# A two-layer hybrid decoder trunk: the low half of every weight tile is formed on GpSimd instead of VectorE

## The chip, the cores and the metric

The kernel runs as one program on one core of a Trainium2 chip. The metric is the device time of one execution in microseconds (us), the median of three runs. Five engines work beside each other, each with its own queue of instructions that it takes strictly in order: TensorE (PE in the profile, with its weight loads as PEld), VectorE (DVE), ScalarE (ACT), GpSimd (POOL) and SyncE (SP), which here only issues DMAs. They wait for each other by semaphores.

## The reference, cut to what matters

Each of the two layers normalises its input, multiplies it by one wide input projection, runs four token mixers on slices of the result (retention, a gated linear recurrence, a diagonal state space with a scan, and a Mamba-2 style recurrence), gates and concatenates the four outputs, and multiplies them by an output projection that is added to the residual. The prompt has 2048 tokens of width 1024; beside it go 8 single tokens with states of their own.

```python
hn = rms_norm(x, norm_w)
proj = (hn @ w_in).astype(f32)            # 1024 x 3332
...                                       # four mixers, 256 columns each
mixed = jnp.concatenate([o_ret, o_hgrn, o_s5, o_m2], axis=-1).astype(x.dtype)
x_out = x + mixed @ w_out                 # 1024 x 1024
```

All of it is float32. The kernel keeps that precision in the two large products by splitting each operand into a high part, rounded to the matmul's reduced float32 type (fp32r), and a low part, the rest: `hi*hi + lo*hi + hi*lo`, three matmuls in place of one.

## The kernel before, in words

The prompt is worked through in blocks of 512 tokens, four to a layer, eight in all. For a block the program runs the input projection in four pieces (`gemm_A`, `gemm_H`, `gemm_M`, `gemm_S`), the mixers (`mix_A`, `mix_H`, `mix_M`, `mix_S`) and the output projection (`out_proj`). The mixers are generators. After each weight tile of a projection the program hands out a few of their steps, so that TensorE's order, which is written out by hand, alternates between a dozen projection matmuls and a mixer's small ones.

The order on the other engines is not written by hand. A scheduler places their instructions by priority and by its own idea of when each is ready; weight tiles have the priority offset `WPRI`, evacuations of finished banks `EPRI`. What a queue holds is fixed when the program is built.

A weight tile comes through a small pipeline, in `gemm` (narrow, lines 606 to 618) and in `gemm_wide` (lines 683 to 691). A DMA fetches 256 KB into a `wr` tile, of which there are 6; ScalarE writes the high half, rounded, into a `wh` tile, of which there are 5; VectorE subtracts the two and writes the low half:

```python
S.copy(hl[:, 0, 0:512], raw[:, 0:512])                        # L688: high half, ScalarE
V.tensor_tensor(hl[:, 1, 0:512], raw[:, 0:512],
                hl[:, 0, 0:512].bitcast(F32), ALU.subtract)   # L689: low half, VectorE
```

There are 296 tiles from `gemm_wide` (L688 and L689) and 248 from `gemm` (L615 and L616), 544 in all. TensorE uses a tile in 12 or 24 matmuls on lines 695, 633 and 628. Both inputs of the subtraction lie in SBUF, as does its output.

GpSimd has little to do before the change. The letters in `GS = 'rpdmwf'` choose what it does: the sums of the rotary embedding in `gemm_A` (L1133 and L1134, four pairs to a block), a product and the diagonals at the start of `mix_H` (L1270, L1281), two products in `mix_S` (L1452 and L1455), the decay masks of `mix_M` (L1585, eight to a block), and parts of the set-up of a layer (L299, L303). Everything else elementwise is VectorE's: it reads the finished banks (tiles `gb` and `mb` in PSUM), and runs the chains of the mixers, the inverse square roots (L227 to L233) among them. The buffers named `half` and `big` are shared by all mixers.

Of the kernel before, what the change touches and what calls it, by code (L numbers as in the profile page):

```python
# [11 lines left out]
F32 = mybir.dt.float32  # L12
# [4 lines left out]
ALU = mybir.AluOpType  # L17
# [96 lines left out]
def trunk_kernel(ctx: ExitStack, tc: tile.TileContext, A: dict):  # L114
    nc = tc.nc
    V, G, S, T = nc.vector, nc.gpsimd, nc.scalar, nc.tensor
# [29 lines left out]
    def nm(s):  # L146
        uid[0] += 1
        return f"{s}_{uid[0]}"
# [32 lines left out]
    def mbank():  # L181
        return mps.tile([P, 512], F32, name=nm("mb"), tag="mb")
# [415 lines left out]
    def gemm(lhs, w, c0, mode, evac, dec=None, tail=None, ks=(0, 1, 2, 3), late=False):  # L598
        n = 256 + (4 if tail is not None else 0)
        per = 2 if (mode == "T" and tail is None) else 1  # L600
        nb = 4 if tail is not None else 2
        banks = [gps.tile([P, 512], F32, name=nm("gb"), tag="gb") for _ in range(nb)]
        dbank = mbank() if dec is not None else None
        raws, hls = [], []

        def load(ki):
            k2 = ks[ki]
            with tc.high_priority(offset=WPRI):
                hl = whp.tile([P, 2, 2, 260], F32R, name=nm("wh"), tag="wh")
                raw = wrp.tile([P, 2, 260], F32, name=nm("wr"), tag="wr")  # L610
                rows = w[2 * k2 * P : 2 * (k2 + 1) * P].rearrange("(k p) c -> p k c", p=P)
                nc.sync.dma_start(raw[:, :, 0:256], rows[:, :, c0 : c0 + 256])
                if tail is not None:
                    nc.sync.dma_start(raw[:, :, 256:260], rows[:, :, tail : tail + 4])
                S.copy(hl[:, 0, :, :n], raw[:, :, :n])  # L615
                V.tensor_tensor(hl[:, 1, :, :n], raw[:, :, :n], hl[:, 0, :, :n].bitcast(F32), ALU.subtract)  # L616
            hls.append(hl)
            raws.append(raw)

        def out(i):  # L620
            with tc.high_priority(offset=EPRI):
                evac(i, banks[i][:, 0 : per * 256].rearrange("p (t c) -> p t c", t=2) if per == 2 else banks[i])

        def t_pass(ki, tt):
            for k in range(2):
                o = banks[tt // per][:, (tt % per) * 256 : (tt % per) * 256 + n]
                for pi, (a, c) in enumerate(((1, 0), (0, 1), (0, 0))):
                    T.matmul(o, lhs[2 * ks[ki] + k][:, a, tt * P : (tt + 1) * P], hls[ki][:, c, k, :n],  # L628
                             start=(ki == 0 and k == 0 and pi == 0 and tt % per == 0), stop=(ki == 3 and k == 1 and pi == 2 and tt % per == per - 1))

        def f_pass(ki, k, i):
            for pi, (a, c) in enumerate(((1, 0), (0, 1), (0, 0))):
                T.matmul(banks[i], hls[ki][:, a, k, i * P : (i + 1) * P], lhs[2 * ks[ki] + k][:, c, :],  # L633
                         start=(ki == 0 and k == 0 and pi == 0), stop=(ki == 3 and k == 1 and pi == 2))

        def dec_pass(ki):
            for j in range(4 if dec is not None else 0):
                T.matmul(dbank[32 * j : 32 * j + 8, :n], dec[0]()[:, 2 * ks[ki - 1 + j // 2] + j % 2, :], raws[ki - 1 + j // 2][:, j % 2, :n],
                         start=(ki == 1), stop=(ki == 3))

        if late:
            for ki in range(4):
                load(ki)
            for tt in range(4):
                for ki in range(4):
                    t_pass(ki, tt)
                if tt % per == per - 1:
                    out(tt // per)
                if tt == 3:
                    for ki in (1, 3):  # L650
                        dec_pass(ki)
                    if dec is not None:
                        dec[1](n, dbank)
                yield
            return
        for ki in range(4):
            load(ki)
            if mode == "T":
                for tt in range(4):
                    t_pass(ki, tt)  # L660
                    if ki == 3 and tt % per == per - 1:
                        out(tt // per)
            elif ki < 3:
                for k in range(2):
                    for i in range(2):
                        f_pass(ki, k, i)
            else:
                for i in range(2):
                    for k in range(2):
                        f_pass(ki, k, i)  # L670
                    out(i)
            if ki % 2 == 1:
                dec_pass(ki)
            if ki == 3 and dec is not None:
                dec[1](n, dbank)
            yield

    def gemm_wide(lhs, w, c0, evac, dec=None, ks=tuple(range(KT)), pre=None, lead=2):
        banks = [gps.tile([P, 512], F32, name=nm("gb"), tag="gb") for _ in range(4)]
        dbank = mbank() if dec is not None else None  # L680
        raws, hls = [], []

        def load(kt):
            with tc.high_priority(offset=WPRI):
                hl = whp.tile([P, 2, 520], F32R, name=nm("wh"), tag="wh")
                raw = wrp.tile([P, 520], F32, name=nm("wr"), tag="wr")
                nc.sync.dma_start(raw[:, 0:512], w[ks[kt] * P : (ks[kt] + 1) * P, c0 : c0 + 512])
                S.copy(hl[:, 0, 0:512], raw[:, 0:512])  # L688
                V.tensor_tensor(hl[:, 1, 0:512], raw[:, 0:512], hl[:, 0, 0:512].bitcast(F32), ALU.subtract)  # L689
            raws.append(raw)  # L690
            hls.append(hl)

        def t_pass(kt, tt):
            for pi, (a, c) in enumerate(((1, 0), (0, 1), (0, 0))):
                T.matmul(banks[tt], lhs[ks[kt]][:, a, tt * P : (tt + 1) * P], hls[kt][:, c, 0:512],  # L695
                         start=(kt == 0 and pi == 0), stop=(kt == KT - 1 and pi == 2))

        def dec_pass(kt):
            if dec is not None and kt % DW == DW - 1:
                for k in range(kt - DW + 1, kt + 1):  # L700
                    j = k % 4
                    T.matmul(dbank[32 * j : 32 * j + 8, :], dec[0]()[:, ks[k], :], raws[k][:, 0:512], start=(k < 4), stop=(k >= 4))

        for kt in range(KT - 2):
            load(kt)
            for tt in range(4):
                t_pass(kt, tt)
            dec_pass(kt)
            if pre is not None and lead and kt >= KT - 2 - lead:
                pre(kt - KT + 2 + lead)  # L710
            yield
        load(KT - 2)
        load(KT - 1)
        for tt in range(4):
            t_pass(KT - 2, tt)
            t_pass(KT - 1, tt)
            with tc.high_priority(offset=EPRI):
                evac(tt, banks[tt])
            if pre is not None and lead and tt + lead < 4:
                pre(tt + lead)  # L720
            if tt == 1:
                yield
        dec_pass(KT - 2)
        dec_pass(KT - 1)
        if dec is not None:
            dec[1](512, dbank)
        yield
# [394 lines left out]
    def gemm_A(L, B):  # L1122
# [27 lines left out]
        def ev2(tt, ps):  # L1150
            S.copy(B.rv[:, tt, :], ps[:, 0:256])
            S.activation(B.rg[:, tt, :], ps[:, 256:512], AF.Silu)

        yield from gemm_wide(B.hn, w, C_RV, ev2, dec=B.dec and B.dec.chunk("rv"))
        yield from gemm_wide(B.hn, w, C_RQ, ev1, dec=dec, pre=pre1)

    def mix_A(L, B):
# [895 lines left out]
```

## Time and profile before

| | |
|---|---|
| time, median of 3 runs | 2244.28 us (2241.43 to 2245.09) |
| the profiled execution | 2245.02 us, its span 2243.2 us |
| TensorE busy | 2118.9 us, 94% |
| VectorE busy | 1669.3 us, 74% |
| ScalarE busy | 1034.2 us, 46% |
| GpSimd busy | 239.5 us, 11% |
| mean granted TensorE clock | 0.98 |

The span runs from the first to the last instruction of the profile; 1.8 us of the execution lie outside it. A share of busy time says how much of the span an engine was executing; the time in which its queue stood still because the instruction at its head was waiting does not count as busy, and the view of waits shows it instead.

### The profile page before, as it was taken

How to read it: one execution, taken by the hardware profiler on the slowest of the kernel's cores; microseconds unless marked ns; L12 is line 12 of the kernel's file. 1: busy time of each engine (PE TensorE's matmuls, PEld its weight loads, DVE VectorE, ACT ScalarE, POOL GpSimd, SP SyncE). 2: the span in 40 equal slices, each digit the busy share in tenths (PEclk: the TensorE clock that was granted, in tenths of full speed). 3: DMA queues.
4: the chain of work that ended last, by engine and by line, in shares of the span. 5: the costliest groups of instructions: out<-in, count | busy, mean ns of one | idle time of the engine just before them, and what ended most of it. 6: DMA issues, size and time to landing. Idle time of an engine off the chain costs nothing. (4 is left out here: it accounts for less than half of the span.)

```text
span 2243.2 us, 41062 instructions
## 1 busy us (share of the span) xinstructions
PE 2118.9 (94%) x15031; PEld 1712.8 (76%) x15031; DVE 1669.3 (74%) x4614; ACT 1034.2 (46%) x1889; POOL 239.5 (11%) x212
## 2 busy tenths in 40 slices
PE   7999989999999999999999998999899899999996
PEld 7778767776777877788877876777677678878786
DVE  6888666898749977787747867489985687748774
ACT  7434433456333564346453453444634245454343
POOL 0112011000210002201100011000120001100100
PEclk9999999999999999999999999999999999999999
DMA  6324633236524364374533335334652253431272
GB/s 213 104 66 120 182 104 118 90 108 203 143 67 143 94 196 121 115 167 126 179 97 112 95 113 165 99 109 119 202 154 78 86 163 101 156 92 50 68 260 94
DMA packets 263354, 284.41 MB, mean 127 GB/s; under 512 B 88752, under 2 KB 183616, under 8 KB 263152
## 3 DMA queue, kind: packets, MB, share of 16 engines
q1 hardware_dynamic: 263152, 281.79, 42.4%
q8 instruction: 118, 1.93, 0.4%
q14 instruction: 84, 0.69, 0.1%
HBM read 245.52 MB, written 31.99 MB: 124 GB/s over the span
## 5 line engine op out<-in xcount | busy, mean ns | idle before, releaser
L695 PE MATMUL gb<-wh,hn 128*128 128x512 f32 x2208 | 542.1, 400 | 3.4 <-DVE half L1650 2.3
L633 PE MATMUL gb<-hn,wh 128*128 128x512 f32 x1920 | 485.9, 406 | 10.3 <-DVE wh L616 6.9
L695 PEld LDWEIGHTS gb<-wh,hn 128*128 128x128 f32 x2208 | 409.9, 188 | 109.1 <-issue 11.6
L633 PEld LDWEIGHTS gb<-hn,wh 128*128 128x128 f32 x1920 | 359.9, 192 | 99.2 <-DVE wh L616 8.1
L689 DVE TENSOR_TENSOR wh<-wr,wh 128x512 fp32r<-128x512 f32 x296 | 215.3, 732 | 242.6 <-ACT wh L688 239.2
L688 ACT CAST wh<-wr 128x512 fp32r<-128x512 f32 x296 | 183.2, 620 | 373.5 <-PE gb L695 193.6
L695 PE MATMUL gb<-wh,mx 128*128 128x512 f32 x1344 | 341.5, 407 | 7.9 <-DVE half L1733 5.8
L695 PEld LDWEIGHTS gb<-wh,mx 128*128 128x128 f32 x1344 | 251.3, 192 | 77.8 <-DVE half L1733 10.1
L615 ACT CAST wh<-wr 128x512 fp32r<-128x512 f32 (+1 forms) x248 | 152.3, 619 | 308.4 <-PE gb L633 83.5
L616 DVE TENSOR_TENSOR wh<-wr,wh 128x512 fp32r<-128x512 f32 (+1 forms) x248 | 183.3, 745 | 77.6 <-ACT wh L615 74.2
L628 PE MATMUL gb<-wh,hn 128*128 128x256 f32 (+1 forms) x1728 | 220.2, 286 | 11.1 <-DVE convc L1524 4.7
L628 PEld LDWEIGHTS gb<-wh,hn 128*128 128x128 f32 x1728 | 211.6, 191 | 15.8 <-issue 9.2
L1585 POOL TENSOR_TENSOR half<-mats,m_lal 128x512 fp32r<-128x512 f32 x64 | 75.5, 1198 | 829.1 <-DVE m_lal L1579 278.8
L1330 DVE COPY_PREDICATED big<-lvl,mb 64x256 f32<-64x256 int32 x192 | 95.3, 537 | 2.5
L1297 ACT COPY zbH<-big 64x512 f32<-64x512 f32 x112 | 70.8, 632 | 48.5 <-PE mb L1306 35.9
L1523 DVE SCALAR_TENSOR_TENSOR big<-gb,vt,big 128x511 f32<-128x511 f32 (+2 forms) x96 | 71.1, 743 | 3.9 <-ACT big L1521 3.5
L1306 PE MATMUL mb<-zbH,big 128*64 128x64 f32 x1536 | 56.9, 229 | 11.0 <-DVE half L1177 5.3
L1306 PEld LDWEIGHTS mb<-zbH,big 128*64 128x64 f32 x1536 | 50.8, 142 | 20.5 <-issue 15.4
L1281 POOL TENSOR_TENSOR big<-mats,h_dg 128x1024 f32<-128x1024 f32 x16 | 30.7, 1942 | 241.8 <-DVE h_dg L1278 197.6
L1482 PE MATMUL mb<-big,big 128*64 128x128 f32 x512 | 40.6, 307 | 15.1 <-DMA big<-s5c 14.7
L628 PE MATMUL gb<-wh,mx 128*128 128x256 f32 x384 | 47.3, 282 | 4.7 <-DVE mx L1505 2.8
L1482 PEld LDWEIGHTS mb<-big,big 128*64 128x64 f32 x512 | 33.6, 155 | 23.7 <-issue 17.0
(497 smaller groups left out, 3091.2 us busy)
## 6 DMA issues: line engine op xcount, KB each, us to landing
wr<-in_w_in SPq DMA_DIRECT2D x416, 256.0 KB
wr<-in_w_out SPq DMA_DIRECT2D x128, 256.0 KB
big<-s5c SPq DMA_DIRECT2D x64, 256.0 KB
xn<-xmid SPq DMA_DIRECT2D x32, 512.0 KB
xn<-in_x_prompt SPq DMA_DIRECT2D x24, 512.0 KB
big<-s5c SPq DMA_DIRECT2D x24, 512.0 KB
xmid<-half SPq DMA_DIRECT2D x44, 256.0 KB
half<-xmid SPq DMA_DIRECT2D x44, 256.0 KB
```

Of the source, the lines that this page charges most:

```text
L615: S.copy(hl[:, 0, :, :n], raw[:, :, :n])
L616: V.tensor_tensor(hl[:, 1, :, :n], raw[:, :, :n], hl[:, 0, :, :n].bitcast(F32), ALU.subtract)
L628: T.matmul(o, lhs[2 * ks[ki] + k][:, a, tt * P : (tt + 1) * P], hls[ki][:, c, k, :n], start=(ki == 0 and k == 0 and pi == 0 and tt % per = ...
L633: T.matmul(banks[i], hls[ki][:, a, k, i * P : (i + 1) * P], lhs[2 * ks[ki] + k][:, c, :], start=(ki == 0 and k == 0 and pi == 0), stop=(ki ...
L688: S.copy(hl[:, 0, 0:512], raw[:, 0:512])
L689: V.tensor_tensor(hl[:, 1, 0:512], raw[:, 0:512], hl[:, 0, 0:512].bitcast(F32), ALU.subtract)
L695: T.matmul(banks[tt], lhs[ks[kt]][:, a, tt * P : (tt + 1) * P], hls[kt][:, c, 0:512], start=(kt == 0 and pi == 0), stop=(kt == KT - 1 and ...
L1306: T.matmul(ps[su, j * 64 : (j + 1) * 64], k[:, j // 4, (j % 4) * P + 64 * u : (j % 4) * P + 64 * u + 64], qz[:, :, j * 64 + 32 * u : j * 6 ...
L1330: V.copy_predicated(stv[p][su, :, nu * u : nu * u + nu, :], mv, ps[su, p * 256 : p * 256 + 256].rearrange("p (c b h) -> p c b h", c=8, h=h))
L1482: T.matmul(ps[64 * hb : 64 * hb + 64, g4 * P : (g4 + 1) * P], lhs, (tq if i else cq)[:, hb, g4], start=(i == 0), stop=(i == 1))
L1523: V.scalar_tensor_tensor(acc[:, 3 - i :], ps[:, : TB - 3 + i], w(i), acc[:, 3 - i :], ALU.mult, ALU.add)
L1585: E('m').tensor_tensor(mms[tt][i].rearrange("p (h t) -> p h t", h=4), tri[:, None, :].to_broadcast([P, 4, P]), lal[:, i, tt, :][:, :, None ...
```

## The change

The subtraction is issued on `G` (GpSimd) in place of `V` (VectorE), in both places. `split_engine` gives `G` each time. Its six lines move all later lines of the file: L689 before is L695 after, L1133 is L1139, and so on.

```diff
                 S.copy(hl[:, 0, :, :n], raw[:, :, :n])
-                V.tensor_tensor(hl[:, 1, :, :n], raw[:, :, :n], hl[:, 0, :, :n].bitcast(F32), ALU.subtract)
+                G.tensor_tensor(hl[:, 1, :, :n], raw[:, :, :n], hl[:, 0, :, :n].bitcast(F32), ALU.subtract)
...
+    nsplit = [0]
+
+    def split_engine():
+        nsplit[0] += 1
+        return G if True else V
+
...
                 S.copy(hl[:, 0, 0:512], raw[:, 0:512])
-                V.tensor_tensor(hl[:, 1, 0:512], raw[:, 0:512], hl[:, 0, 0:512].bitcast(F32), ALU.subtract)
+                split_engine().tensor_tensor(hl[:, 1, 0:512], raw[:, 0:512], hl[:, 0, 0:512].bitcast(F32), ALU.subtract)
```

TensorE's order stays as it was. VectorE's queue shrinks and the scheduler reorders it a little; GpSimd's queue grows from 212 to 756 instructions. Two places show how.

The first is VectorE's queue inside `mix_M` of the first block. `half_3001` is the decay matrix that L1619 multiplies, `half_3008` the values that L1621 scales for the matmuls of L1632, the `wh` tiles are weights. Before:

```order
L1653 TENSOR_TENSOR half_2983<-half_2983,big_2067 128x256
L689 TENSOR_TENSOR wh_3087<-wr_3088,wh_3087 128x512
L689 TENSOR_TENSOR wh_3092<-wr_3093,wh_3092 128x512
L1619 TENSOR_TENSOR half_3001<-half_3001,half_3005 128x512
L689 TENSOR_TENSOR wh_3149<-wr_3150,wh_3149 128x512
L1621 TENSOR_TENSOR half_3008<-half_2996,m_dt_2345 128x256
L689 TENSOR_TENSOR wh_3189<-wr_3190,wh_3189 128x512
```

And the same place after:

```order
L1659 TENSOR_TENSOR half_2983<-half_2983,big_2067 128x256
L1625 TENSOR_TENSOR half_3001<-half_3001,half_3005 128x512
L1627 TENSOR_TENSOR half_3008<-half_2996,m_dt_2345 128x256
L1628 TENSOR_TENSOR half_3008<-half_3008,m_ec_2526 128x256
L1657 TENSOR_TENSOR half_2996<-half_2996,m2c_446 128x256
```

The three subtractions that stood ahead of L1621 are gone from this queue.

The second place is GpSimd's queue at the end of `gemm_A` and the start of `gemm_H` in the second block. `half_3298` and `half_3299` belong to `mix_S` of the block before, the next eight rows are the rotary sums. Before, these rows followed each other with nothing between:

```order
L1133 TENSOR_TENSOR half_3428<-half_3424,half_3425 128x8x32
L1134 TENSOR_TENSOR half_3428<-half_3424,half_3425 128x8x32
L1452 TENSOR_TENSOR half_3298<-half_3299,big_3294 128x512
L1455 TENSOR_TENSOR half_3299<-half_3299,big_3294 128x512
L1133 TENSOR_TENSOR half_3441<-half_3437,half_3438 128x8x32
L1134 TENSOR_TENSOR half_3441<-half_3437,half_3438 128x8x32
```

And after:

```order
L616 TENSOR_TENSOR wh_3478<-wr_3479,wh_3478 128x2x256
L616 TENSOR_TENSOR wh_3495<-wr_3496,wh_3495 128x2x256
L1458 TENSOR_TENSOR half_3298<-half_3299,big_3294 128x512
L1461 TENSOR_TENSOR half_3299<-half_3299,big_3294 128x512
L1139 TENSOR_TENSOR half_3398<-half_3394,half_3395 128x8x32
L1140 TENSOR_TENSOR half_3398<-half_3394,half_3395 128x8x32
L1139 TENSOR_TENSOR half_3413<-half_3409,half_3410 128x8x32
...
L1139 TENSOR_TENSOR half_3441<-half_3437,half_3438 128x8x32
L1140 TENSOR_TENSOR half_3441<-half_3437,half_3438 128x8x32
L616 TENSOR_TENSOR wh_3516<-wr_3517,wh_3516 128x2x256
```

Two weight tiles now stand ahead of the mixer's products and the rotary sums, and the third tile of `gemm_H`, `wh_3516`, behind all of them.

## Rows read from the trace of the kernel before

**Rows 1.** The page, part 1: busy us, share of the span, instructions.
```profile
PE 2118.9 (94%) x15031; PEld 1712.8 (76%) x15031; DVE 1669.3 (74%) x4614; ACT 1034.2 (46%) x1889; POOL 239.5 (11%) x212
```

**Rows 2.** Waits of PE: line, waited for, us in total, times, longest us.
```profile
PE mb L1482 <- DMA big<-s5c: 14.7, 10, 4.7
PE gb L633 <- DVE wh L616: 6.9, 2, 4.0
...
PE mb L1187 <- DVE half L1177: 0.2, 1, 0.2
```

**Rows 3.** The page, part 5: the subtractions; busy, mean ns, idle before and what ended it.
```profile
L689 DVE TENSOR_TENSOR wh<-wr,wh 128x512 fp32r<-128x512 f32 x296 | 215.3, 732 | 242.6 <-ACT wh L688 239.2
...
L616 DVE TENSOR_TENSOR wh<-wr,wh 128x512 fp32r<-128x512 f32 (+1 forms) x248 | 183.3, 745 | 77.6 <-ACT wh L615 74.2
```

**Rows 4.** Timeline of VectorE, 244.5 to 253.2 us: start, us, line, tiles, idle before.
```profile
245.13 0.41 DVE L1653 TENSOR_TENSOR half<-half,big 128x256 f32<-128x256 f32 x1
248.90 0.69 DVE L689 TENSOR_TENSOR wh<-wr,wh 128x512 fp32r<-128x512 f32 x1 [3.35 <-ACT wh L688]
...
250.45 0.69 DVE L1619 TENSOR_TENSOR half<-half,half 128x512 f32<-128x512 f32 x1
251.85 0.69 DVE L689 TENSOR_TENSOR wh<-wr,wh 128x512 fp32r<-128x512 f32 x1 [0.71 <-ACT wh L688]
252.46 0.42 DVE L1621 TENSOR_TENSOR half<-half,m_dt 128x256 f32<-128x256 f32 x1
```

**Rows 5.** Timeline of PE, 251 to 254 us and 2041 to 2048 us.
```profile
253.02 1.12 PE L1632 MATMUL mb<-half,half 128*64 128x64 f32 x16 [2.78 <-DVE half L1621]
...
2046.32 1.64 PE L628 MATMUL gb<-wh,hn 128*128 128x260 f32 x6 [3.59 <-DVE convc L1524]
```

**Rows 6.** Groups of GpSimd by line and shape: busy us, mean ns, idle before.
```profile
L1585 POOL TENSOR_TENSOR half<-mats,m_lal 128x512 fp32r<-128x512 f32 x64 | 75.5, 1198 | 829.1 <-DVE m_lal L1579 278.8 <-DMA wr<-in_w_in 136.0 <-PE gb L628 124.9
...
L1455 POOL TENSOR_TENSOR half<-half,big 128x512 f32<-128x512 f32 x8 | 14.3, 1794 | 0.6
L1452 POOL TENSOR_TENSOR half<-half,big 128x512 f32<-128x512 f32 x8 | 12.0, 1498 | 276.6 <-DVE half L1443 132.5 <-DMA big<-pd_su 95.6 <-DMA big<-s5c 48.6
```

**Rows 7.** Single lines: durations in ns, shortest/median/longest.
```profile
L1585 POOL TENSOR_TENSOR half<-mats,m_lal x64: 1032/1040/2628, 201.5 to 2111.4; 128x512 fp32r<-128x512 f32 x64
...
L1452 POOL TENSOR_TENSOR half<-half,big x8: 1260/1556/1606, 297.7 to 2161.0; 128x512 f32<-128x512 f32 x8
```

**Rows 8.** Timeline, all engines, 760 to 800 us: four masks on GpSimd beside VectorE.
```profile
776.15 0.18 DVE L299 TENSOR_TENSOR cm_s<-half 128x32 f32<-128x32 f32 x1
776.21 4.05 POOL L1585 TENSOR_TENSOR half<-mats,m_lal 128x512 fp32r<-128x512 f32 x4 [114.48 <-DMA s5c<-big]
776.26 1.06 DVE L302 TENSOR_TENSOR half<-half 128x32 f32<-128x32 f32 x1
...
778.24 1.08 DVE L300 TENSOR_TENSOR half<-half,cm_s 128x32 f32<-128x32 f32 x1
```

**Rows 9.** Timeline, all engines, 297 to 302 us: end of `gemm_A`, start of `gemm_H`.
```profile
297.72 1.26 POOL L1452 TENSOR_TENSOR half<-half,big 128x512 f32<-128x512 f32 x1
297.79 0.69 DVE L1130 TENSOR_TENSOR half<-gb,half 128x512 f32<-128x512 f32 x1 [0.62 <-POOL half L1134]
...
299.06 1.77 POOL L1455 TENSOR_TENSOR half<-half,big 128x512 f32<-128x512 f32 x1
299.62 1.75 DVE L616 TENSOR_TENSOR wh<-wr,wh 128x512 fp32r<-128x512 f32 x1
...
301.43 0.80 PE L633 MATMUL gb<-hn,wh 128*128 128x512 f32 x1 [4.01 <-DVE wh L616]
301.92 1.18 POOL L1134 TENSOR_TENSOR half<-half,half 128x256 f32<-128x256 f32 x1
```

**Rows 10.** The tile `wh`, idle time of the engines that use it: one line.
```profile
  DVE wh L616: 15.0, 5
```

**Rows 11.** Line 1453, which follows the product of L1452: its engine's idle time.
```profile
  POOL half L1452: 6.6, 6
```

## The prediction

> **What bounds the kernel now.** I read the page first. TensorE is busy for 94% of the span, VectorE for 74%, GpSimd for 11% [rows 1]. So the kernel's time is TensorE's stream of matmuls plus the time in which that stream stands still, 2243.2 - 2118.9 = 124.3 us. A change that leaves TensorE's order alone, as this one does, can move only those 124 us, or add to them.
>
> Second I read who ends TensorE's waits. The list has 48 rows that sum to 111.6 us: 38 rows end with a VectorE instruction (77.9 us in 66 waits, the first and the last of these rows shown), 8 with ScalarE (12.8 us), 2 with a DMA (20.9 us, the row of L1482 the larger) [rows 2]. None ends with GpSimd. VectorE is therefore what TensorE waits for, although it is idle for a quarter of the span.
>
> Third, what VectorE does when TensorE waits. Its 544 subtractions take 215.3 + 183.3 = 398.6 us, and before them the engine stood idle for 242.6 + 77.6 = 320.2 us, nearly all of it until ScalarE had written the high half [rows 3]. A queue is taken in order, so in that time nothing behind the subtraction could run. Together the weight work holds VectorE's queue for 719 us, 32% of the span.
>
> The timeline shows what this does to a mixer. L1653 ends at 245.5; then VectorE waits 3.35 us for a cast, subtracts twice, runs L1619, waits 0.71, subtracts, and only then runs L1621 [rows 4], and TensorE has waited 2.78 us for L1621 [rows 5]. A counter-example is the wait of 3.59 us at 2046.32, ended by L1524 [rows 5]: VectorE's timeline has no subtraction in the 8 us before it.
>
> **What the change removes.** From VectorE's queue 398.6 us of work and 320.2 us of waiting at its head. I followed the waits on VectorE back through its timeline for 8 us each, as in [rows 4]; about half of their time has subtractions, or waits for casts, ahead of the instruction that TensorE wanted. So of 77.9 us some 39 us can shrink. A wait does not vanish when one instruction ahead of it goes, since the next producer (the bank that TensorE itself fills, ScalarE's activation) is then the late one; and VectorE gets new delays, below. I take half of the 39: minus 20 us. The bounds are 0 and minus 39.
>
> **What it adds to GpSimd.** No row shows this subtraction on GpSimd. The nearest are other products of 128x512: the masks of L1585, whose two inputs are small or repeated, take 1198 ns in the mean and 1032 at the shortest; L1452 takes 1498 and 1260, L1455 1794 [rows 6, 7]. I take 1.26 us for the work, since L1452 reads two full inputs as the subtraction does, and 1.45 us with waiting: the masks' mean stands 16% above their shortest. That is 544 x 1.45 = 789 us, and GpSimd's load becomes 239.5 + 789 = 1029 us, 46%. The bounds are 544 x 1.03 = 560 and 544 x 1.79 = 974 us, that is 800 to 1213 us in all; even the last leaves the engine idle for close to half of the span. Throughput is not the question, then; latency and VectorE's delays are.
>
> **What it adds to VectorE.** The two engines get in each other's way. While four masks ran on GpSimd, VectorE instructions of the same tiny shape took 1.06 to 1.08 us each, and the one just before 0.18 [rows 8]; a subtraction beside L1455 took 1.75 us [rows 9]. All of these read two operands from SBUF. L1130, which reads one from PSUM, took 0.69 us beside L1452 [rows 9], as long as the same line's instructions without such company. So a GpSimd instruction costs VectorE between 0 (it runs instructions on PSUM, or none) and 0.9 us (it stands in front of one with two SBUF inputs). I take 0.4 us, a little under the middle, because the evacuations, which TensorE mostly waits for, belong to the first kind. 544 x 0.4 = 218 us: VectorE's busy time goes from 1669.3 to 1669.3 - 398.6 + 218 = 1489 us, with 1271 and 1760 as the ends. The 320 us of waiting for casts move to GpSimd's queue. VectorE is the freer for it in the middle case, and hardly at the upper end.
>
> **Weights that come later.** A tile is ready 1.45 - 0.74 = 0.7 us later. With 5 `wh` tiles this is mostly hidden behind the matmuls of the tiles ahead: of 544 subtractions only five of the narrow ones ended an idle time of TensorE or its weight loads, 15.0 us together [rows 10], and two of them matter to the matmuls, 6.9 us [rows 2]. Those two are one place in two layers, shown for the first at 301.43 [rows 9]. There the change acts twice. The subtraction no longer suffers from VectorE, but in GpSimd's new queue `wh_3516` stands behind L1452's and L1455's products and all eight rotary sums. The last of these began at 301.92 and took 1.18 us [rows 9]; with 1.3 us behind it the tile would come at 304.4 in place of 301.4, 3 us later, if the sums are not earlier. Two places make plus 6 us; the bounds are 0 and 5 x 3 = 15.
>
> **GpSimd's other work.** Its 184 older products now stand behind subtractions, and behind casts that are late. VectorE waits for L1452 for 6.6 us already [rows 11]. If such waits double, and TensorE sees under half of that, it is plus 3 us; the bounds are 0 and 16.
>
> **The sum.** The profiled execution took 2245.0 us (span 2243.2 and 1.8 outside). 2245.0 - 20 + 6 + 3 = 2234 us. The median of the runs before, 2244.28, lies 0.03% below that execution, which changes nothing here. The likeliest case by itself runs from 2215 to 2240.
>
> **Rivals.** First, the engines' collision decides and the kernel gets slower. The mechanism: each subtraction on GpSimd stops VectorE's next instruction with two SBUF inputs for the rest of its length, and the chains with many of them (the inverse square roots, the scan, the gates) arrive late at TensorE. For it speak [rows 8], where VectorE lost 0.9 us to each GpSimd instruction. Then 544 x 0.9 = 490 us replace 399, and each of the 66 waits on VectorE grows by about 0.9 us less the half microsecond that its weight work now costs it: 66 x 0.4 = plus 26 us, 2271 us. It decides as soon as a subtraction costs VectorE more than the 0.73 us that it used to take there. Against it: the waits for casts, 320 us, leave that queue in any case.
>
> The Trainium skill takes this side. Its page "Perfetto Trace Analysis", section "Optimizing Scalar/DVE Operations", warns that work moved between these two engines "might not help" because they share a read port of SBUF, and the page "SBUF — State Buffer", section "Who interferes with whom", says that the one that starts first keeps it for its whole instruction. The trace agrees with the second as far as [rows 8, 9] go, L1130's exception included; whether the first follows, no row of before can say, and it is the rival just priced.
>
> Second, nothing that can be measured: what VectorE gains ahead of TensorE's waits it loses to GpSimd, or the waits that subtractions lie in front of are ended a moment later by something else, as 33.7 us of the waits are already (ScalarE and DMAs). Then the gain is some 5 us and the costs are the 9 us above or less: 2243 to 2249 us, say 2246.
>
> Third, the gain is larger: all 39 us go, `wh_3516` comes no later because a freer VectorE starts the rotary sums earlier, and the costs stay at 3: 2245 - 39 + 3 = 2209 us.
>
> That the change does not do what it says is not among them: the queues above show all the moved rows.
>
> **How the numbers follow.** The forecast, 2234, has a chance of 0.42; the larger gain 0.11; no change 0.19; slower by collision 0.28. The range of 2205 to 2272 us leaves out the far ends of the first rival and of the third, about one in five. What a measurement of this kernel can tell from no change is about 0.2%, 4.5 us. Faster by more than that: 0.53, the forecast and the larger gain; within it: 0.19; slower: 0.28.
>
> **What would show each step.** The subtraction on GpSimd at 1.3 to 1.5 us in the mean, and GpSimd's busy time near 1030 us. VectorE's busy time near 1490 us: 1271 would mean no collisions, over 1670 the first rival. The waits for casts in front of GpSimd's rows. TensorE's waits on VectorE at 55 to 60 us rather than 78, the wait at L1632 gone, the one ended by L1524 still there. A wait of L633 for `wh` at the start of the second block's `gemm_H` of 4 to 7 us. I am wrong if VectorE is clearly freer and TensorE's waits do not fall, or if TensorE's waits for weights grow in many places, which would mean that GpSimd's queue, and not its speed, sets when weights come.

## The result and the profile after

The kernel became slower: 2305.54 us (median of 4 runs, 2300.03 to 2318.83) against 2243.23 us (2241.43 to 2245.09) on the same chip. The ratio is 1.0286, with an interval of 1.0240 to 1.0333. The forecast was 2234 us with a range of 2205 to 2272: wrong in sign, and outside the range.

The profiled execution after is the longest of its four, 2318.83 us, so its span overstates the loss: 2317.1 - 2243.2 = 74 us, where the medians differ by 62. Part 1 of the page after, against [rows 1]:

```profile
span 2317.1 us, 41172 instructions
PE 2150.9 (93%) x15031; PEld 1734.0 (75%) x15031; DVE 1579.8 (68%) x4070; ACT 1031.9 (45%) x1889; POOL 951.6 (41%) x756
```

TensorE runs the same 15031 matmuls, yet it is busy for 32 us longer (2150.9 against 2118.9) and idle for 42 us longer (166.2 against 124.3). So the loss has two parts, waits and slower matmuls. VectorE is freer by 89.5 us, and this didn't help. The list of TensorE's waits, in the rows that answer to [rows 2] (us in total, times, longest):

```profile
PE gb L633 <- POOL wh L616: 10.4, 3, 4.4
PE gb L701 <- DVE half L1739: 10.2, 7, 3.2
PE gb L628 <- DVE big L1532: 7.5, 6, 1.8
...
PE mb L559 <- DVE big L554: 6.9, 1, 6.9
```

The list has 55 rows with 153.0 us, where the one before had 48 with 111.6. VectorE's part rose from 77.9 to 103.7 us, ScalarE's from 12.8 to 24.5; GpSimd, which ended no wait before, has 10.7; DMA fell from 20.9 to 12.9. The subtraction itself, in the list of GpSimd's groups (busy, mean ns, idle before), which answers to [rows 3]:

```profile
L695 POOL TENSOR_TENSOR wh<-wr,wh 128x512 fp32r<-128x512 f32 x296 | 401.8, 1365 | 705.9 <-ACT wh L694 599.9 <-DMA wr<-in_w_in 32.7 <-issue 29.3
L616 POOL TENSOR_TENSOR wh<-wr,wh 128x512 fp32r<-128x512 f32 (+1 forms) x248 | 333.2, 1352 | 509.5 <-ACT wh L615 479.7 <-DMA wr<-in_w_in 16.1 <-DMA wr<-in_w_out 4.9
```

It takes 1.36 us, and the waits for casts now stand in front of GpSimd, as forecast.

Where VectorE loses is plainest at the start of the program, because the instructions there are tiny and known. VectorE's timeline after (start, us, line, tiles, count of instructions):

```profile
7.86 0.16 DVE L233 SCALAR_TENSOR_TENSOR nf_rs<-rs,nf_rs 128x1 f32<-128x1 f32 x1
...
8.06 1.37 DVE L231 TENSOR_TENSOR rs<-nf_rs 128x1 f32<-128x1 f32 x2
9.35 1.30 DVE L232 TENSOR_TENSOR rs<-rs,rs 128x1 f32<-128x1 f32 x2
10.58 1.30 DVE L233 SCALAR_TENSOR_TENSOR nf_rs<-rs,nf_rs 128x1 f32<-128x1 f32 x2
11.80 1.83 DVE L554 TENSOR_SCALAR big<-big,nf_rs 128x1024 f32<-128x1024 f32 x1
```

GpSimd's timeline of the same stretch:

```profile
8.15 4.93 POOL L616 TENSOR_TENSOR wh<-wr,wh 128x512 fp32r<-128x512 f32 x4 [3.85 <-ACT wh L615]
```

And TensorE's, with the wait in brackets:

```profile
13.68 0.69 PE L559 MATMUL mb<-mats,big 128*128 128x128 f32 x2 [6.90 <-DVE big L554]
```

Four subtractions run from 8.15 to 13.08. In that time VectorE gets through one pair of instructions per subtraction: L231, L232 and L233 need 0.16 us for one instruction, and 1.3 us for two. Taken one by one, the second of each pair ends at 9.43, 10.65 and 11.87, and the first three subtractions at 9.41, 10.64 and 11.86. L554 ends at 13.63, and TensorE has stood still for 6.90 us. The same stretch before, VectorE first, TensorE in the second fence:

```profile
8.70 0.22 DVE L233 SCALAR_TENSOR_TENSOR nf_rs<-rs,nf_rs 128x1 f32<-128x1 f32 x2
8.84 0.68 DVE L616 TENSOR_TENSOR wh<-wr,wh 128x512 fp32r<-128x512 f32 x1
9.44 0.74 DVE L554 TENSOR_SCALAR big<-big,nf_rs 128x1024 f32<-128x1024 f32 x1
```

```profile
10.24 1.97 PE L559 MATMUL mb<-mats,big 128*128 128x128 f32 x8 [3.83 <-DVE big L554]
```

A subtraction in front of VectorE's chain cost it 0.7 us; one beside the chain on GpSimd costs 1.1 us (1.30 against 0.22 for the pair of L233), since the blocked instruction ends only with it.

In the middle of the program TensorE mostly waits for an instruction that isn't itself blocked: 80.5 of its 103.7 us of waits on VectorE end with one that reads PSUM. In one such place VectorE's order is the same before and after. After, VectorE first, then GpSimd, then TensorE:

```profile
1538.72 0.72 DVE L232 TENSOR_TENSOR rs<-rs,rs 128x8 f32<-128x8 f32 x1
...
1540.24 1.25 DVE L233 SCALAR_TENSOR_TENSOR hp_rs<-rs,hp_rs 128x8 f32<-128x8 f32 x1
...
1542.28 0.69 DVE L1739 TENSOR_TENSOR half<-half,gb 128x512 f32<-128x512 f32 x1
```

```profile
1538.13 1.30 POOL L695 TENSOR_TENSOR wh<-wr,wh 128x512 fp32r<-128x512 f32 x1 [7.42 <-ACT wh L694]
1540.21 1.26 POOL L695 TENSOR_TENSOR wh<-wr,wh 128x512 fp32r<-128x512 f32 x1 [0.78 <-ACT wh L694]
```

```profile
1543.02 0.80 PE L701 MATMUL gb<-wh,mx 128*128 128x512 f32 x1 [3.20 <-DVE half L1739]
```

And before:

```profile
1480.57 0.15 DVE L232 TENSOR_TENSOR rs<-rs,rs 128x8 f32<-128x8 f32 x1
...
1481.52 0.17 DVE L233 SCALAR_TENSOR_TENSOR hp_rs<-rs,hp_rs 128x8 f32<-128x8 f32 x1
...
1482.47 0.69 DVE L1733 TENSOR_TENSOR half<-half,gb 128x512 f32<-128x512 f32 x1
```

```profile
1483.22 1.68 PE L695 MATMUL gb<-wh,mx 128*128 128x512 f32 x6 [1.55 <-DVE half L1733]
```

L1739 reads a finished bank in PSUM and takes 0.69 us in both. It comes late because two tiny instructions of an inverse square root, L232 and L233, stand ahead of it in VectorE's queue and are 0.57 and 1.08 us longer beside the subtractions; TensorE's wait grows by 1.65 us.

The slower matmuls are mostly the clock. Another stall ends at 94.36:

```profile
94.36 1.86 PE L1312 MATMUL mb<-zbH,big 128*64 128x64 f32 x32 [4.89 <-DVE h_t L1327]
```

Windows of the profile after around it (length; busy us and count of PE, PEld, DVE, ACT, POOL; granted clock; DMA share; GB/s):

```profile
89.00:94.00 5.00, 0.48 (x3) 0.04 (x1) 5.00 (x20) 1.16 (x3) 0.91 (x1) 1.00 0.39 111
94.00:98.00 4.00, 3.63 (x36) 3.20 (x37) 4.00 (x9) 1.31 (x2) 3.64 (x3) 0.57 0.33 82
98.00:102.00 4.00, 4.00 (x19) 3.24 (x18) 3.97 (x6) 1.17 (x3) 4.00 (x4) 1.00 0.48 139
```

After 4.89 us in which TensorE waited for L1327 the granted clock is 0.57 in the next window, mostly the lower of its two levels (1.2 and 2.4 GHz), and then full again. Over the whole span the view of cores gives:

```profile
core 0: 2317.1 us, clock 0.965
```

It was 0.980 before. By an estimate from these means, the time lost to the lower level is 0.035 x 2317.1 = 81 us after and 0.020 x 2243.2 = 45 us before; the difference, 36 us, is close to the 32 us by which TensorE's busy time grew.

### The profile page after: what moved, and what is told of

It is laid out like the page before. It is cut to its first block, busy times and chain, and to the rows that moved or that the text cites. A ratio compares the mean times of both kernels' runs of the same rounds, so it can differ in the third digit from the quotient of the medians.

```text
span 2317.1 us, 41172 instructions
## 1 busy us (share of the span) xinstructions
PE 2150.9 (93%) x15031; PEld 1734.0 (75%) x15031; DVE 1579.8 (68%) x4070; ACT 1031.9 (45%) x1889; POOL 951.6 (41%) x756
## 5 line engine op out<-in xcount | busy, mean ns | idle before, releaser
L695 POOL TENSOR_TENSOR wh<-wr,wh 128x512 fp32r<-128x512 f32 x296 | 401.8, 1365 | 705.9 <-ACT wh L694 599.9
L701 PE MATMUL gb<-wh,hn 128*128 128x512 f32 x2208 | 548.9, 404 | 2.0 <-DVE half L1656 0.8
L616 POOL TENSOR_TENSOR wh<-wr,wh 128x512 fp32r<-128x512 f32 (+1 forms) x248 | 333.2, 1352 | 509.5 <-ACT wh L615 479.7
L633 PE MATMUL gb<-hn,wh 128*128 128x512 f32 x1920 | 494.4, 411 | 25.7 <-POOL wh L616 10.4
L701 PEld LDWEIGHTS gb<-wh,hn 128*128 128x128 f32 x2208 | 415.3, 191 | 109.2 <-issue 9.4
L633 PEld LDWEIGHTS gb<-hn,wh 128*128 128x128 f32 x1920 | 365.4, 195 | 117.6 <-issue 13.9
L628 PEld LDWEIGHTS gb<-wh,hn 128*128 128x128 f32 x1728 | 214.7, 194 | 21.4 <-issue 14.0
L1183 DVE TENSOR_TENSOR half<-mb,mats 128x256 f32<-128x256 f32 x64 | 24.5, 419 | 98.3 <-PE mb L1180 92.0
L1591 POOL TENSOR_TENSOR half<-mats,m_lal 128x512 fp32r<-128x512 f32 x64 | 69.8, 1107 | 35.3 <-DVE m_lal L1585 18.7
L743 DVE SCALAR_TENSOR_TENSOR mx<-mb,vt,mx 128x512 fp32r<-128x512 f32 x48 | 35.6, 743 | 47.3 <-ACT mx L742 46.9
L1499 DVE TENSOR_TENSOR big<-big,big 128x1024 f32<-128x1024 f32 x8 | 9.8, 1226 | 73.6 <-ACT big L1497 73.6
```

The costliest lines, as they stand in the source:

```text
L616: G.tensor_tensor(hl[:, 1, :, :n], raw[:, :, :n], hl[:, 0, :, :n].bitcast(F32), ALU.subtract)
L695: split_engine().tensor_tensor(hl[:, 1, 0:512], raw[:, 0:512], hl[:, 0, 0:512].bitcast(F32), ALU.subtract)
L1591: E('m').tensor_tensor(mms[tt][i].rearrange("p (h t) -> p h t", h=4), tri[:, None, :].to_broadcast([P, 4, P]), lal[:, i, tt, :][:, :, None ...
```

## The experiments

Eleven kernels were run. Three theories stood against each other: GpSimd's reads block VectorE (C); weights come late through GpSimd's queue (W); the scheduler's other order does it (R). The kernels ran in three groups, each on a chip of its own, and each time is compared with the kernel before in the same group: 2243.76 us for e1 to e4, 2241.0 for e5 to e8, 2240.73 for e9 to e11. TensorE's 15031 matmuls come in the same order in the kernels before and after and in e1, e2, e3, e7 and e8.

**No low half at all** (e1_no_low). Nobody subtracts, and the low part of the weights is missing from the result.

```diff
-                V.tensor_tensor(hl[:, 1, :, :n], raw[:, :, :n], hl[:, 0, :, :n].bitcast(F32), ALU.subtract)
-                            T.matmul(o, ..., hls[ki][:, c, k, :n],
+                            T.matmul(o, ..., hls[ki][:, 0, k, :n],
...
```

> Starts from the kernel before. The subtraction is left out and the matmuls read the high half where they read the low one, so the low part of the weights is missing from the result; the number of matmuls is the same. It shows what taking the weight work off VectorE is worth with nothing put on GpSimd. Theory C (the two engines collide over reads from SBUF): VectorE is freed of 399 us and of the waits for casts and gets nothing back: 2215 to 2230 us. Rival W (weights come late through GpSimd's queue): the same, since no weight waits for a subtraction: 2215 to 2230. Rival R (the scheduler's other order on VectorE, ScalarE and SyncE is what costs): the order of the change without its subtractions, so still slow, 2270 to 2300.

2166.26 us, ratio 0.9666 (0.9641 to 0.9690): 77.5 us, some four times the relief that I had priced, and well below the 2215 to 2230 expected. Its page, its cores and its largest waits:

```profile
PE 2089.3 (97%) x15031; PEld 1694.8 (78%) x15031; DVE 1320.9 (61%) x4070; ACT 1034.8 (48%) x1889; POOL 219.6 (10%) x212
```

```profile
core 0: 2162.4 us, clock 0.992
```

```profile
PE mb L542 <- DMA mats<-in_c_mats: 6.8, 1, 6.8
PE gb L693 <- DVE half L1731: 5.7, 7, 1.5
PE gb L627 <- DVE convc L1522: 4.2, 2, 2.7
PE mb L1480 <- DMA big<-s5c: 3.8, 4, 1.8
```

TensorE's idle time falls by 51 us, from 124.3 to 73.1. Its list of waits falls from 111.6 to 61.1 us: VectorE's part from 77.9 to 34.7, and DMA's from 20.9 to 10.6 too, since L1480's loads into `big` (L1482 in [rows 2]) are no longer waited for as long. Its busy time falls by 30 us; the clock, 0.980 to 0.992, gives 45 - 17 = 28 by the same estimate.

**GpSimd subtracts, nobody reads** (e2_unread). The changed kernel, with TensorE's matmuls reading the high half in place of the low.

```diff
+                G.tensor_tensor(hl[:, 1, :, :n], raw[:, :, :n], hl[:, 0, :, :n].bitcast(F32), ALU.subtract)
-                            T.matmul(o, ..., hls[ki][:, c, k, :n],
+                            T.matmul(o, ..., hls[ki][:, 0, k, :n],
...
```

> Starts from the changed kernel. GpSimd subtracts as there, but the matmuls read the high half instead of the low one, so that TensorE waits for no subtraction; the low part of the weights is missing from the result. Theory C: all collisions stay, so the time stays near the changed kernel's, 2285 to 2305 us, with VectorE busy near 1580 us. Rival W: TensorE no longer waits for weights through GpSimd, so the time falls to that of the kernel without a low half, 2215 to 2235.

2299.43 us (2295.27 to 2306.63), 1.0258 (1.0221 to 1.0295). As C said. No matmul waits for a subtraction here, and all but some 6 us of the loss is still there: W is refuted as the main cause. Against the run without subtractions the only work added is GpSimd's, and it costs 2299.43 - 2166.26 = 133 us. The order is not what differs: the traces of the two have VectorE's 4070 instructions in the same place of the queue in 3935 cases, so R is no cause of the 133 us. They go through VectorE: from the run without subtractions to this one, TensorE's list of waits grows from 61.1 to 143.1 us, VectorE's part of it from 34.7 to 98.0, ScalarE's from 14.8 to 30.4, and GpSimd ends none; TensorE's busy time grows by 55 us (2089.3 to 2144.4), with the mean granted clock at 0.969 in place of 0.992.

**Memsets on GpSimd** (e3_memset). In place of each subtraction three memsets of the same tile, which read nothing.

```diff
-                V.tensor_tensor(hl[:, 1, :, :n], raw[:, :, :n], hl[:, 0, :, :n].bitcast(F32), ALU.subtract)
+                for _ in range(3):
+                    G.memset(hl[:, 1, :, :n].bitcast(F32), 0.0)
...
```

> Starts from the kernel before. In place of the subtraction GpSimd fills the low half with zeros, three times over (about 1.4 us a tile), and the matmuls read it: TensorE depends on GpSimd's queue as in the changed kernel, GpSimd is busy as long, but reads nothing for it. The low part of the weights is missing from the result. Theory C: without reads the weight work does not stop VectorE; VectorE busy near 1270 to 1330 us, time 2215 to 2240. Rival W: weights still come through GpSimd's queue, so the time stays near 2290 to 2305.

2174.55 us, 0.9700 (0.9676 to 0.9724): 8 us above the run without subtractions, though GpSimd is busier than in the changed kernel (1062.1 us against 951.6). A GpSimd that is busy but reads nothing costs little; one that reads costs much. C was right in kind; that it expected 2215 to 2240 comes from the relief, which I still took too small. R is left with little: VectorE's instructions stand in the same place as without subtractions in 4000 of 4070 cases. Nor is it GpSimd's older products, which now queue behind the weight work: VectorE waits for GpSimd for 74.6 us in this run and for 74.6 us in the one before it, which is 125 us slower.

**GpSimd copies the raw tile** (e7_copy). One operand is read in place of two.

```diff
-                V.tensor_tensor(hl[:, 1, 0:512], raw[:, 0:512], hl[:, 0, 0:512].bitcast(F32), ALU.subtract)
+                G.tensor_copy(hl[:, 1, 0:512], raw[:, 0:512])
...
```

> As in the run in which GpSimd subtracts and nobody reads the low halves, but GpSimd copies the raw tile (one operand read) instead of subtracting (two operands read). TensorE's matmuls read the high half in place of the low. If any read of SBUF by GpSimd blocks VectorE's two-operand instructions for as long as it lasts, the loss scales with how long the copy takes: at half the length of the subtraction about 2235, at its full length about 2300; so 2230 to 2300 us and VectorE's two-operand instructions at 830 to 945 us of busy time. If it takes GpSimd reading two operands to block VectorE, the time is that of the memsets, 2170 to 2190, and VectorE is busy about 1360 us.

2191.32 us (2185.75 to 2193.69), 0.9772 (0.9743 to 0.9802): 25 us above the run without subtractions, or 28 when each is taken from the kernel before of its own group (49.7 below it, against 77.5). It lies just above the range for "it takes two operands" and far below that for "any read blocks for as long as it lasts", so a read of one operand does block, but little. The copy takes half the time of the subtraction, from GpSimd's groups:

```profile
L689 POOL CAST wh<-wr 128x512 fp32r<-128x512 f32 x296 | 197.4, 668 | 868.1 <-PE gb L695 356.3 <-DMA wr<-in_w_in 137.7 <-PE gb L633 137.3
```

What the four runs did to VectorE is best read from two groups of its instructions, by shape (busy, mean ns, idle before). One (`big<-big,h_t`) reads two operands from SBUF, the other (`half<-mb,mats`) reads one of its two from PSUM (`mb`). Nobody subtracts:

```profile
L1175 DVE TENSOR_TENSOR half<-mb,mats 128x256 f32<-128x256 f32 x64 | 24.5, 420 | 99.8 <-PE mb L1172 99.4
L1318 DVE TENSOR_TENSOR big<-big,h_t 128x256 f32<-128x256 f32 x48 | 21.1, 444 | 18.4 <-PE mb L1311 10.0 <-PE mb L1304 8.2
```

GpSimd subtracts:

```profile
L1326 DVE TENSOR_TENSOR big<-big,h_t 128x256 f32<-128x256 f32 x48 | 30.9, 659 | 6.8 <-PE mb L1312 3.9 <-PE mb L1319 2.6
...
L1183 DVE TENSOR_TENSOR half<-mb,mats 128x256 f32<-128x256 f32 x64 | 24.5, 419 | 93.9 <-PE mb L1180 87.4 <-ACT wh L694 6.2
```

GpSimd sets memory:

```profile
L1322 DVE TENSOR_TENSOR big<-big,h_t 128x256 f32<-128x256 f32 x48 | 21.4, 451 | 17.5 <-PE mb L1315 9.5 <-PE mb L1308 7.8
```

GpSimd copies:

```profile
L1320 DVE TENSOR_TENSOR big<-big,h_t 128x256 f32<-128x256 f32 x48 | 21.9, 463 | 16.0 <-PE mb L1313 9.3 <-PE mb L1306 6.5
```

The PSUM form stays at 419 to 420 ns beside subtractions and with nobody subtracting; the SBUF form goes from 444 to 659 beside subtractions, and to 451 and 463 beside memsets and copies. The durations of all 4070 instructions in the four traces, summed by kind (us), show that this holds for the whole engine, and that memsets are not without effect:

| | nobody | subtracts | memsets | copies |
|---|---|---|---|---|
| 1297 with an input in PSUM | 612.0 | 610.6 | 612.4 | 611.2 |
| 581 copies, casts and scalings (COPY, CAST, TENSOR_SCALAR) without one | 131.7 | 179.6 | 180.9 | 143.8 |
| 2192 others without one | 770.9 | 985.6 | 783.0 | 828.4 |

In sum, copies, casts and scalings are slowed by memsets as much as by subtractions. One of them, with nobody subtracting and beside memsets:

```profile
L1659 DVE TENSOR_SCALAR half<-half,m_rs 128x256 f32<-128x256 f32 x32 | 10.0, 350 | 0.5
```

```profile
L1663 DVE TENSOR_SCALAR half<-half,m_rs 128x256 f32<-128x256 f32 x32 | 17.0, 568 | 0.5
```

But the memset run pays 8 us in all; what comes with the 133 us is the last row, 215 us longer beside subtractions and 12 beside memsets. VectorE's busy time from part 1 of the pages says the same for the whole engine: 1320.9 without subtractions, and then

```profile
PE 2144.4 (93%) x15031; PEld 1729.4 (75%) x15031; DVE 1578.7 (69%) x4070; ACT 1033.8 (45%) x1889; POOL 961.4 (42%) x756
```

```profile
PE 2097.1 (96%) x15031; PEld 1700.9 (78%) x15031; DVE 1356.6 (62%) x4070; ACT 1034.6 (48%) x1889; POOL 1062.1 (49%) x1844
```

```profile
PE 2101.9 (96%) x15031; PEld 1703.9 (78%) x15031; DVE 1392.3 (64%) x4070; ACT 1034.8 (47%) x1889; POOL 579.9 (26%) x756
```

with subtractions, memsets and copies: plus 258, 36 and 71 us for the same 4070 instructions, and plus 133, 8 and 25 us of time. The order of the three is the same in both. The Trainium skill, page "SBUF — State Buffer", section "Who interferes with whom", states that VectorE's instructions with two SBUF inputs contend with a GpSimd instruction that reads SBUF and not with one that only writes it. The rows of L1318 agree: 659 ns beside subtractions, which read, and 451 beside memsets, which only write, where it is 444 with neither. How much less a copy costs than a subtraction (463), the rows show, and no run here says why.

**VectorE subtracts, nobody reads** (e8_v_unread). Is the 77 us of the first run VectorE's time, or TensorE's wait for the low halves?

```diff
-                            T.matmul(o, ..., hls[ki][:, c, k, :n],
+                            T.matmul(o, ..., hls[ki][:, 0, k, :n],
...
```

> VectorE forms every low half as in the kernel before, but TensorE's matmuls read the high half in place of the low, so that no matmul waits for a subtraction. If what the run without subtractions gained (77 us) is VectorE's time (401 us taken out of its queue), this kernel stays near the one before: 2228 to 2246 us. If the gain is the wait of TensorE for the low halves, it comes back here: 2166 to 2190 us. Before, the waits of TensorE for a low half from VectorE were 6.9 us in all, which speaks for the first.

2243.53 us, 0.9999 (0.9982 to 1.0016). The wait is worth nothing; the 77 us come from taking the subtractions out of VectorE's queue. Two things go together there: the time, and the order that the scheduler then gives the rest. With the weight work left out, 2386 of VectorE's 4070 instructions stand in the same place without subtractions as before, and nine in ten have moved by at most 8 places; so it is more than the little that the section on the change says. What the order alone is worth was not tested.

**Only the wide tiles, only the narrow tiles** (e4_wide, e5_narrow).

```diff
 # e4_wide: gemm_wide alone
-                V.tensor_tensor(hl[:, 1, 0:512], ...)
+                G.tensor_tensor(hl[:, 1, 0:512], ...)
 # e5_narrow: gemm alone
-                V.tensor_tensor(hl[:, 1, :, :n], ...)
+                G.tensor_tensor(hl[:, 1, :, :n], ...)
```

> Half of the change: the 296 subtractions of the wide tiles are on GpSimd, the 248 of the narrow ones stay on VectorE. Theory C: 296 of 544 collisions, so 54% of the 62 us: 2270 to 2285 us. Rival W: in the changed kernel TensorE waits 10.4 us for the narrow tiles of line 616 and 0.3 us for the wide ones, so the loss sits with the narrow tiles and this half costs next to nothing: 2240 to 2255.

> Only the 248 subtractions of the narrow tiles go to GpSimd; the 296 of the wide tiles stay on VectorE. The theory that GpSimd's reads block VectorE (C) prices this by two rates that the first four runs gave: each microsecond of subtraction taken from VectorE is worth 77.5 / 401 = 0.19 us of the kernel, each microsecond for which VectorE's other instructions are blocked costs 133 / 266 = 0.50 us. By these the wide half should have cost +12.5 us, and it cost 10.4. For the narrow half, 186 us go and 266 - 108 = 157 us of blocking come: -36 + 79 = +43, so 2280 to 2295 us, with VectorE about 1640 us busy. By the count of subtractions alone (the rival: each costs the same) it would be 248/544 of +62 = +28 us, 2265 to 2277. That weights come late through GpSimd's queue (W) would put nearly the whole loss here, 2295 to 2306, with TensorE's added waits ended by GpSimd.

Wide: 2254.2 us, 1.0056 (1.0034 to 1.0079). Narrow: 2281.9 us, 1.0181 (1.0150 to 1.0213). The first expectation of C, by the count, was wrong: 296 wide tiles cost 10 us and 248 narrow ones 41. By the time for which VectorE's single instructions ran longer than their kind does undisturbed (108 us in the wide run, summed over all instructions, of 266 in all), C priced the narrow run before it ran at +43. The blocking there came near its forecast (VectorE's instructions without a PSUM input take 150 us more than before, where 157 were forecast), and VectorE was busy for 1665.9 us, where 1640 were. In the narrow run a weight wait shows as well, the largest of its list:

```profile
PE gb L633 <- POOL wh L616: 14.2, 3, 6.5
```

It was 6.9 in 2 times before [rows 2]; so some 7 of the 41 us may be W's.

**A later rank for the subtraction** (e6_late25). On VectorE as before, behind the mixers' work where both are ready.

```diff
+            with tc.high_priority(offset=25):
                 V.tensor_tensor(hl[:, 1, 0:512], raw[:, 0:512], hl[:, 0, 0:512].bitcast(F32), ALU.subtract)
...
```

> As the kernel before, with the subtractions on VectorE, but ranked 75 places later in the scheduler's order (an offset of 25 in place of 100), so that mixers' instructions that TensorE waits for go ahead of them. If a good part of the 77 us that VectorE's relief is worth lies in the subtractions that stand just ahead of such instructions, 2215 to 2238 us. The rival: the instructions that stand ahead wait for TensorE anyway and the rows move by a few places only, so nothing changes (2238 to 2250), or the weights come late and TensorE waits for them (2250 to 2275).

2234.72 us, 0.9981 (0.9963 to 1.0000): at the edge of what can be told from no change. It lies in the range for "a good part of the 77 us", but 6 us are no good part of them; that range was too wide to tell.

**Some of the wide calls on GpSimd** (e9_pick, e11_worst), and the first choice with the later rank (e10_pick_late).

```diff
+        E = G if ncall[0] in (2, 4, 5, 10, 14, 15, 19, 20, 24, 25, 29, 30, 34) else V   # e9, e10
+        E = G if ncall[0] in (0, 1, 3, 11, 23, 27, 31, 35, 36) else V                   # e11
+        ncall[0] += 1
...
-                V.tensor_tensor(hl[:, 1, 0:512], ...)
+                E.tensor_tensor(hl[:, 1, 0:512], ...)
```

> Of the 37 calls of the wide GEMM, the 13 in whose stretch a subtraction on GpSimd blocked VectorE for less than 0.2 us on average (read from the trace of the run with all wide tiles on GpSimd) give their 104 subtractions to GpSimd; all others stay on VectorE. If the place decides (C with the two rates): 104 x 0.73 = 76 us leave VectorE, worth 76 x 0.19 = 14.7; about 10 us of blocking come, costing 5: minus 9 us, 2230 to 2238, a little faster than the kernel before. If the loss goes by the count of subtractions on GpSimd, 104/296 of the +10 of the wide half: 2242 to 2248.

> The opposite choice: the nine calls in whose stretch a subtraction on GpSimd blocked VectorE for over 0.6 us on average (72 subtractions, mean some 0.75 us). If the place decides: 72 x 0.73 = 53 us leave VectorE (-10), 54 us of blocking come (+27): plus 17 us, 2252 to 2264, with fewer subtractions on GpSimd than in the run of the 13 calls. If the count decides: 72/296 of +10, 2241 to 2247.

> The 13 calls on GpSimd and the later rank of the subtractions (an offset of 25) together, as a version that may beat both kernels. If the two gains add (-9 forecast, -6 measured for the rank alone): 2224 to 2232 us. If both shorten the same waits: 2230 to 2240.

The 13 calls with little blocking: 2240.95 us, 1.0000 (0.9984 to 1.0015), where C said -9. The nine with much: 2234.43 us, 0.9980 (0.9963 to 0.9998), where C said +17 and the count of subtractions 0 to +6. Both expectations of C missed, and for the nine calls the sign as well. The blocking itself came about as forecast: the instructions of VectorE without a PSUM input took 11 us longer than before in the first run and 42 in the second (912.9 and 943.7 against 901.6), where 10 and 54 were forecast. Its price did not. So the two rates (0.19 us per microsecond taken from VectorE, 0.50 per microsecond of blocking) describe the runs with some 250 subtractions or more, and not those with single calls: blocking somewhere in a call's stretch does not say that TensorE waits behind it. What decides at doses of 70 to 100 stays open. The combination ran at 2235.03 us, 0.9968 (0.9952 to 0.9984): by 0.3% the one version whose interval stays well clear of no change, but its median is that of the later rank alone (2234.72) and of the nine calls (2234.43), and the three can't be told apart.

## Why the prediction was wrong

The parts, as measured: relief -77.5 (no low half), blocking +133.2 (GpSimd subtracts, unread), waiting for the low half from GpSimd +6.1 (2305.54 - 2299.43, two medians whose ranges meet), together +61.8. That this comes to the measured +62.3 is no proof of the parts, since each is the difference between one run and the next.

**The step that failed** is the collision's price for TensorE. I put 218 us of it on VectorE's busy time, but in the sum, -20 + 6 + 3, it has no term; at most it is part of why I halved the relief from 39 to 20, as if VectorE, still freer than before on balance, could hide its delays. It measured 258 us on VectorE, or 0.47 us for each subtraction in place of 0.4, so that size was nearly right; but it cost 133 us of the kernel's time.

My reason was that the evacuations, which TensorE mostly waits for, read PSUM and aren't blocked. Both are true: instructions that read PSUM kept their time (612.0 and 610.6 us), and in the traces they end 47.9 of the 77.9 us of waits on VectorE before. What I missed is that they stand in one queue behind instructions that are blocked, as L1739 does at 1542.28. TensorE's waits that end with a VectorE instruction that reads PSUM are 24.9 us without subtractions and 71.5 with GpSimd subtracting unread; those that end with another one, 9.6 and 26.3.

Nor is a microsecond of VectorE's busy time worth the same wherever it falls: 77.5 / 398.6 = 0.19 us of the kernel for each microsecond of subtraction that left the queue, 133 / 258 = 0.52 for each that blocking added. That a subtraction often stood where the engine would have waited anyway, and that blocking falls on the mixers' chains, is the likely reason; no run here separates it, and for 72 and 104 subtractions neither rate held.

**The relief**, -20 with bounds of 0 and -39, was -77.5. I had counted only the half of the waits on VectorE that have a subtraction within 8 us ahead, and halved that for what would be late next. Counted over the whole trace, it is two thirds: 52 of the 77.9 us have a subtraction that ended within 8 us before the end of the awaited instruction. The waits on VectorE fell by 43 us, and DMA's by 10 with them; that the loads into shared buffers went out sooner is likely but not shown. And I left out the clock: a long stall can be followed by matmuls at the lower level, as at 94.36, and then costs more than its length. By the estimate above it is 28 of the 77 us here, and 36 of the 74 between the two profiled executions.

**The base for VectorE's busy time** was off as well. Without the subtractions it is 1320.9 us and not 1669.3 - 398.6 = 1271, since neighbouring instructions overlap and the busy time counts such moments once: the durations of VectorE's other 4070 instructions add up to 1512.9 us before and 1514.6 without subtractions. 1489 was forecast, 1579.8 came; 1321 + 258 accounts for it.

**Right:** the subtraction's duration (1.36 us against 1.45 and bounds of 1.03 and 1.79) and GpSimd's load (951.6 against 1029 us); the waits for casts in front of GpSimd; the wait of L1632 for VectorE, which is gone; the one ended by L1524 (now L1530), which is still there (5.7 us in 2 waits); and `wh_3516`, whose wait at the start of `gemm_H` is 4.4 us at its longest, where 4 to 7 were forecast. "Weights later", +6, is of the size of the +6.1 above, which is within the noise; TensorE's own list has 10.7 us of waits for subtractions in place of 6.9.

**GpSimd's other work**, +3, rested on VectorE's waits for GpSimd doubling. They grew from 16.0 to 68.2 us, 46.8 of it in four waits of L1277 for the product of L1276 in `mix_H`, and the wait for L1458 (L1452 before) only from 6.6 to 7.9. TensorE sees little of it: the memset run has 74.6 us of such waits and pays 8 us in all.

**The first rival** named the mechanism, with a chance of 0.28, and its condition: more than 0.73 us for each subtraction. That condition was wrong: the collision decided at 0.47, because the condition weighed a microsecond of blocking like one of subtraction. And its price, +26, came from 0.4 us on each of 66 waits, with no clock. The sign that I set for being wrong, "VectorE is clearly freer and TensorE's waits do not fall", is what the profile shows: 1579.8 against 1669.3 us, and 103.7 against 77.9.

## What to carry to other kernels

Before moving work with SBUF operands from VectorE to GpSimd, ask which of VectorE's remaining instructions read only SBUF, and what stands behind them in its queue: an evacuation that isn't blocked itself still comes late. With all 544 subtractions moved, each microsecond of blocking cost more than twice what a microsecond of the moved work had; with a few calls moved, no such price could be seen. An engine's freed busy time is no gain by itself: find the price of its time by a run that leaves the work out, before deciding where to put it. Add to a stall of TensorE what the clock does after it.

## What the runs showed of the hardware

- Beside the subtractions VectorE's 1297 instructions that read PSUM kept their time (610.6 us in sum, 612.0 without), while a pair of tiny ones with SBUF inputs took 1.30 us in place of 0.22 (L233 at the start of the program).
- Instructions with one tile as input are caught as well: L554, a scaling of 128x1024 from SBUF, took 1.83 us beside a subtraction and 0.74 before.
- GpSimd's memsets slowed VectorE's 581 copies, casts and scalings from SBUF from 131.7 to 180.9 us, as much as its subtractions did (179.6), and the 2192 others without a PSUM input by 12 us, where the subtractions did by 215.
- A copy of 128x512 takes GpSimd 668 ns, about half of the subtraction's 1365, and costs VectorE 71 / 544 = 0.13 us each in place of 0.47: a good deal less than half.
- GpSimd's 1632 memsets, 529 ns each in the group below, cost VectorE 36 us of busy time in all:

```profile
L691 POOL MEMSET wh<- 128x512 f32 x888 | 463.5, 529 | 570.5 <-PE gb L697 379.2 <-PE gb L634 114.1 <-ACT big L1154 19.9
```
